# A grouped 3x3 convolution on one core: row sizes of loads and stores, whole-image stores, and semaphores cleared during the stores

## The chip, the cores and the metric

The kernel runs on one core of a Trainium2 chip. The metric is the time of one execution on the device in microseconds. Most executions of one kernel agree within about 0.3%, so a change of less than 1% needs several rounds on the same chip.

## The reference

The reference is a convolution with 16 images, 64 input channels, 128 output channels, 64 x 64 pixels, a 3 x 3 window and 8 groups, all in fp32:

```python
x_pad = np.pad(x, ((0, 0), (0, 0), (pad, pad), (pad, pad)))
for g in range(groups):                # 8 groups: 8 channels in, 16 out
    for b in range(batch):             # 16 images
        for co in range(c_out_per_group):
            for ci in range(c_in_per_group):
                for kh in range(k):
                    for kw in range(k):
                        output[b, g*16 + co] += weight[g*16 + co, ci, kh, kw] * x_pad[b, g*8 + ci, kh:kh+h, kw:kw+w]
```

It reads 16.8 MB and writes 33.6 MB.

## The kernel before

The input is loaded from GpSimd's queue with a cast from fp32 to bf16, two images to a tile of 128 partitions, 16 KB of input to a row. TensorE runs nine taps for every block of the output into PSUM. DVE and ACT evict the banks in turn into output buffers, and SyncE stores them. Two "pipes" of eight images each share TensorE. A pipe works on an image pair `i` in four sets `s`, each a quarter of both images, and the second pipe runs half a set behind the first. The prediction calls the four images that both pipes work on at a time a group. The parts that the change touches:

```python
ob = [pool.tile([128, HALF], FP32, name=f"ob{i}") for i in range(NOB)]   # NOB = 16, half images
...
for h0, h1 in ((0, 32), (32, 64)):          # the first tiles come in halves
    if h0 > 0:
        load(xn[0], 0, 0, 128, h0, h1)
    load(xs[0], 544, 0, 128, h0, h1)
    ...
    load(xs[3], 512 - 96, 96, 128, h0, h1)
for i in range(1, 4):                        # the others whole: 16 KB read per row
    load(xn[i], 128 * i, 0, 128, 0, H)
    load(xs[i], 544 + 128 * i, 0, 128 if i < 3 else 96, 0, H)
...
    def finish(self, st):                    # after a set's last tap
        i, s = st // 4, st % 4
        if s % 2 == 0:                       # a new pair of half-image buffers
            self.slots = [(nob[0] + im) % NOB for im in range(2)]
            ...
        for j in range(2):
            for im in range(2):
                ...
                eng.wait((stored[slot], 16 * uses[slot]) if uses[slot] else raw_read, self.full[j, im])
                free[b] = eng.done(copy(ob[slot][:, o0 : o0 + 512], banks[b]))
        if s % 2 == 1:
            s0 = HALF * (s // 2)
            for im in range(2):
                SP.wait(*self.wrote[im])
                nc.sync.dma_start(outf[img][:, s0 : s0 + HALF], ob[slot]).then_inc(stored[slot], 16)
...
SP.wait(*((stored[s], 16 * uses[s]) for s in range(NOB)))     # all stores landed
POOL.wait(SP.done(nc.sync.nop()))
nc.clear_and_free_semaphores(sems)
```

## Time and profile before

| | before |
|---|---|
| median time | 129.51 us (129.28 to 129.68) |
| span of the profiled execution | 127.9 us |
| TensorE busy | 86.4 us, its last eviction over at 97.5 us |
| loads end | 53 us |
| last DMA packet, last store landed | 126.1 us, 126.5 us |
| from the last landing to the end | 1.38 us |

The main lines of the page, of the DMA view and of the windows stand in the prediction. The view of waits says who waited for whom (us in total, times, longest). The evictions waited for TensorE only, never for a store to give its buffer back:

```profile
ACT ob L267 <- PE bank L240: 51.1, 33, 3.9
DVE ob L267 <- PE bank L240: 45.2, 33, 4.7
```

The chain of waits in order of time (start, duration, what) ends 30 us before the kernel does. Its last pieces:

```profile
58.98 30.89 PE bank L240 x793
89.86 0.03 issue
89.89 6.30 PE bank L240 x155
96.19 0.02 issue
96.21 1.29 DVE ob L267 x2
```

The stores that run from there on are missing from it, which is why the slice table must be read first.

### The profile page before, as it was taken

The numbers are of one execution on the slowest core, as the hardware profiler recorded it, in microseconds if no ns is written. First come the engines' busy times: TensorE is split into PE (matmuls) and PEld (weight loads), VectorE is DVE, ScalarE is ACT, GpSimd is POOL, SyncE is SP. The second block draws the span as 40 slices with busy tenths as digits, with TensorE's granted clock in tenths as the row PEclk, the third lists the DMA queues.
The fourth block names the chain that finished last, engine by engine and source line by source line (L and its number), as shares of the span: only waits on it lengthen the run. The fifth ranks groups of instructions, "written<-read, shape, count | busy, mean of one in ns | idle before, by whom it ended". The sixth has DMA issues, their size and how long they took to land.

```text
span 127.9 us, 3812 instructions
## 1 busy us (share of the span) xinstructions
PE 86.4 (68%) x2322; PEld 40.5 (32%) x1170; DVE 45.9 (36%) x74; ACT 39.0 (30%) x70; POOL 6.7 (5%) x18
## 2 busy tenths in 40 slices
PE   0029999999999979999999999999991000000000
PEld 0025435445445434553454543344340000000000
DVE  0174164456446544464544654456444000000000
ACT  4063153354345333353434533444333000000000
POOL 5950000000000000000000000000000000000000
PEclk9999999999999999999999999999999855555555
DMA  3999999999999999999999999999999999999930
GB/s 76 326 213 214 223 218 213 205 264 289 269 287 287 282 287 274 395 423 423 423 418 423 425 412 430 412 430 415 420 423 428 430 423 436 418 428 433 418 143 10
DMA packets 6271, 42.74 MB, mean 334 GB/s; under 512 B 848, under 2 KB 848, under 8 KB 1296
## 3 DMA queue, kind: packets, MB, share of 16 engines
q1 hardware_dynamic: 4752, 34.61, 65.2%
q0 software_dynamic: 1360, 7.87, 30.1%
q8 instruction: 13, 0.21, 0.6%
q10 hardware_dynamic: 144, 0.04, 0.2%
q14 instruction: 2, 0.02, 0.0%
HBM read 16.81 MB, written 33.55 MB: 394 GB/s over the span
## 4 chain that ended last, share of the span: by engine, by line
PE 66%; DVE 4%; DMA 4%; issue 1%; ACTq 0%; DVEq 0%; SPq 0%
PE bank L240 65%; DMA w_sb<-in_weight_dram 4%; DVE E L162 2%; DVE ob L267 2%; PE bank L175 2%; ACTq L329 0%; DVEq L75 0%; SPq L53 0%
## 5 line engine op out<-in xcount | busy, mean ns | idle before, releaser
L240 PE MATMUL bank<-xs,wS 32*64 32x504 bf16 (+3 forms) x1152 | 72.1, 373 | 0.9 <-issue 0.9
L240 PE MATMUL bank<-xn,wN 32*64 32x504 bf16 (+3 forms) x1152 | 70.9, 376 | 0.2 <-DVE ob L267 0.2
L267 DVE COPY ob<-bank 128x512 f32<-128x512 f32 x64 | 41.3, 686 | 45.2 <-PE bank L240 45.2
L267 ACT COPY ob<-bank 128x512 f32<-128x512 f32 x64 | 34.5, 588 | 51.1 <-PE bank L240 51.1
L235 PEld LDWEIGHTS <-wS 32*64 32x64 bf16 x576 | 27.0, 104 | 21.5 <-issue 10.9
L235 PEld LDWEIGHTS <-wN 32*64 32x64 bf16 x576 | 19.4, 105 | 24.9 <-issue 20.7
L175 PE MATMUL bank<-ident,E 128*128 128x128 bf16 x18 | 2.1, 313 | 8.8 <-DVE E L162 8.8
L175 PEld LDWEIGHTS bank<-ident,E 128*128 128x128 bf16 x18 | 1.8, 148 | 8.8 <-DVE E L162 8.8
L162 DVE TENSOR_TENSOR E<-w_sb,mask 128x288 bf16<-128x288 f32 x5 | 2.9, 653 | 4.6 <-DMA w_sb<-in_weight_dram 4.6
L106 POOL DMA_DIRECT2D xs<-in_x_dram x7 | 4.0, 571 | 1.0 <-SPq L53 1.0
L122 ACT CAST xn<-ob 128x1024 bf16<-128x1024 f32 x2 | 2.0, 1042 | 4.1 <-DMA ob<-in_x_dram 4.1
L106 POOL DMA_DIRECT2D xn<-in_x_dram x4 | 2.3, 580 | 0.0
L185 ACT CAST wS<-bank 128x512 bf16<-128x512 f32 (+1 forms) x3 | 1.2, 487 | 1.7 <-PE bank L175 1.7
L185 DVE CAST wN<-bank 128x512 bf16<-128x512 f32 (+1 forms) x3 | 1.5, 551 | 0.7 <-PE bank L175 0.7
L122 ACT ACT_TABLE_LOAD x1 | 1.3, 1283 | 1.4 <-SPq L53 1.4
L129 DVE MEMSET mask<- 128x8 f32 x1 | 0.1, 65 | 1.1 <-SPq L53 1.1
L142 POOL TENSOR_SCALAR_AFFINE_SELECT ident<-ident 128x128 bf16<-128x128 bf16 x1 | 0.3, 303 | 0.0
L137 POOL TENSOR_SCALAR_AFFINE_SELECT mask<-mask 128x8 f32<-128x8 f32 x1 | 0.2, 209 | 0.1
L147 POOL TENSOR_SCALAR_AFFINE_SELECT mask<-mask 128x8 f32<-128x8 f32 x1 | 0.2, 196 | 0.0
L315 POOL MEMSET const-float32-0.0<- 128x1 f32 x1 | 0.1, 98 | 0.3 <-issue 0.3
L130 DVE MEMSET ident<- 128x64 uint32 x1 | 0.1, 112 | 0.0
L315 POOL MEMSET const-bfloat16-1.0<- 128x1 bf16 x1 | 0.1, 101 | 0.0
(2 smaller groups left out, 0.2 us busy)
## 6 DMA issues: line engine op xcount, KB each, us to landing
out_dram<-ob SPq DMA_DIRECT2D x32, 1024.0 KB, 27.2
xn<-in_x_dram POOLq DMA_DIRECT2D x3, 1024.0 KB, 27.2
xs<-in_x_dram POOLq DMA_DIRECT2D x2, 1024.0 KB, 27.1
ob<-in_x_dram SPq DMA_DIRECT2D x1, 1024.0 KB, 5.7
xs<-in_x_dram POOLq DMA_DIRECT2D x2, 512.0 KB, 9.3
xs<-in_x_dram POOLq DMA_DIRECT2D x1, 768.0 KB, 46.0
xn<-in_x_dram POOLq DMA_DIRECT2D x1, 512.0 KB, 9.0
xs<-in_x_dram POOLq DMA_DIRECT2D x2, 128.0 KB, 9.0
```

What stands on the lines that cost most here:

```text
L106: nc.gpsimd.dma_start(t.rearrange("p h w -> p (h w)")[p0:p1, h0 * W : h1 * W], xr[row0 + p0 : row0 + p1, h0 * W : h1 * W],).then_inc(s, 16)
L122: raw_read = ACT.done(nc.scalar.copy(xn[0][:, h : h + 16, :].rearrange("p h w -> p (h w)"), raw[:, h * W : (h + 16) * W],))
L137: m3 = POOL.done(nc.gpsimd.affine_select(out=mask, in_=mask, compare_op=ALU.is_ge, fill=0.0, base=0, channel_multiplier=1, pattern=[[-COg, ...
L142: m4 = POOL.done(nc.gpsimd.affine_select(out=ident, in_=ident, compare_op=ALU.not_equal, fill=1.0, base=0, channel_multiplier=1, pattern=[ ...
L147: m5 = POOL.done(nc.gpsimd.affine_select(out=mask, in_=mask, compare_op=ALU.is_ge, fill=0.0, base=COg - 1, channel_multiplier=-1, pattern= ...
L162: e = DVE.done(nc.vector.tensor_mul(E[:, :, 32 * r : 32 * r + 32].rearrange("p t (g c) -> p t g c", c=CIg), wv.unsqueeze(2).to_broadcast([ ...
L175: ins = nc.tensor.matmul(banks[b][:, 128 * t : 128 * t + 128], E[:, t0 + t, off : off + 128], ident, start=True, stop=True,)
L185: free[b] = eng.done(copy(dst, banks[b][:, 0 : 128 * n]))
L235: pe.ldweights(w_ap, **pos)
L240: ins = pe.add_instruction(mybir.InstMatmult(name=nc.get_next_instruction_name(), engine=mybir.EngineType.PE, start_tensor_calc=k == 0, st ...
L267: free[b] = eng.done(copy(ob[slot][:, o0 : o0 + 512], banks[b]))
L315: nc = _bacc.Bacc("TRN2", target_bir_lowering=False, num_devices=1)
```

## The change

The loads of all tiles go in half images, so a row reads 8 KB and not 16. The stores go in whole images (16 KB rows), except for the first image pair of each pipe, which is still stored in halves so that stores begin early. The output buffers become eight whole images, with the same bytes. At the end, the other semaphores are cleared while the last stores are on their way; SyncE then waits for each store's semaphore and subtracts its value. TensorE's, DVE's and ACT's instructions keep their order. The intent is fewer and larger store rows, a larger share of the engines for the stores while loads run, and less to do after the last store.

```diff
--- before.py
+++ after.py
@@ -33,15 +33,14 @@
     NCH = H // R
     HALF = HW // 2
 
-    HALF = HW // 2
-    NOB = 16
+    NOB = 8
 
     pool = ctx.enter_context(tc.tile_pool(name="sb", bufs=1))
     psum = ctx.enter_context(tc.tile_pool(name="psum", bufs=1, space=bass.MemoryType.PSUM))
 
     xn = [pool.tile([128, H, W], BF16, name=f"xn{i}") for i in range(4)]
     xs = [pool.tile([128, H, W], BF16, name=f"xs{i}") for i in range(4)]
-    ob = [pool.tile([128, HALF], FP32, name=f"ob{i}") for i in range(NOB)]
+    ob = [pool.tile([128, HW], FP32, name=f"ob{i}") for i in range(NOB)]
     w_sb = pool.tile([128, CIg * T], FP32, name="w_sb")
     mask = pool.tile([128, G], FP32, name="mask")
     ident = pool.tile([128, 128], BF16, name="ident")
@@ -112,7 +111,7 @@
                 landed[t.name, q, h] = (s, 16)
 
 
-    raw = ob[NOB - 1]
+    raw = ob[NOB - 1][:, 0:HALF]
     s_raw = sem("raw")
     nc.sync.dma_start(raw, xr[0:128, 0:HALF]).then_inc(s_raw, 16)
     s_w = sem("w")
@@ -150,8 +149,9 @@
             ))
         load(xs[3], 512 - 96, 96, 128, h0, h1)
     for i in range(1, 4):
-        load(xn[i], 128 * i, 0, 128, 0, H)
-        load(xs[i], 544 + 128 * i, 0, 128 if i < 3 else 96, 0, H)
+        for h0, h1 in ((0, 32), (32, 64)):
+            load(xn[i], 128 * i, 0, 128, h0, h1)
+            load(xs[i], 544 + 128 * i, 0, 128 if i < 3 else 96, h0, h1)
 
 
 
@@ -192,7 +192,7 @@
     outf = out.rearrange("b co h w -> b co (h w)")
     taps = [(1, 1)] + [(a, b) for a in range(3) for b in range(3) if (a, b) != (1, 1)]
     pe = nc.tensor
-    stored = [sem(f"st{i}") for i in range(NOB)]
+    stored = [nc.alloc_semaphore(f"st{i}") for i in range(NOB)]
     uses = [0] * NOB
     nob = [0]
     nev = [0]
@@ -253,28 +253,29 @@
 
         def finish(self, st):
             i, s = st // 4, st % 4
-            if s % 2 == 0:
+            if s == 0:
                 self.slots = [(nob[0] + im) % NOB for im in range(2)]
+                self.empty = [(stored[slot], 16 * uses[slot]) if uses[slot] else raw_read for slot in self.slots]
                 self.wrote = [[], []]
                 nob[0] += 2
             for j in range(2):
                 for im in range(2):
                     slot, b = self.slots[im], self.banks[j][im]
-                    o0 = 512 * (2 * (s % 2) + j)
+                    o0 = 512 * (2 * s + j)
                     eng, copy = ((ACT, nc.scalar.copy), (DVE, nc.vector.tensor_copy))[nev[0] % 2]
                     nev[0] += 1
-                    eng.wait((stored[slot], 16 * uses[slot]) if uses[slot] else raw_read, self.full[j, im])
+                    eng.wait(self.empty[im], self.full[j, im])
                     free[b] = eng.done(copy(ob[slot][:, o0 : o0 + 512], banks[b]))
                     self.wrote[im].append(free[b])
                 nev[0] += 1
             nev[0] += 1
-            if s % 2 == 1:
-                s0 = HALF * (s // 2)
+            if s == 1 and i == 0 or s == 3:
+                o0, o1 = (0 if s == 1 or not (i == 0) else HALF), HALF * (s + 1) // 2
                 for im in range(2):
                     slot = self.slots[im]
                     img = 2 * i + 8 * self.k + im
                     SP.wait(*self.wrote[im])
-                    nc.sync.dma_start(outf[img][:, s0 : s0 + HALF], ob[slot]).then_inc(stored[slot], 16)
+                    nc.sync.dma_start(outf[img][:, o0:o1], ob[slot][:, o0:o1]).then_inc(stored[slot], 16)
                     uses[slot] += 1
 
     pipes = (Pipe(0), Pipe(1))
@@ -293,9 +294,20 @@
                 p.finish(st)
 
 
-    SP.wait(*((stored[s], 16 * uses[s]) for s in range(NOB)))
+
     POOL.wait(SP.done(nc.sync.nop()))
     nc.clear_and_free_semaphores(sems)
+
+    for n in range(nob[0], nob[0] + NOB):
+        s = stored[n % NOB]
+        num = dict(sync_type="semaphore", id=s.num, ant_name=s.name)
+        nc.sync.add_instruction(mybir.InstEventSemaphore(
+            name=nc.get_next_instruction_name(), engine=mybir.EngineType.SP,
+            sync_info=mybir.SyncInfo(
+                on_wait=[mybir.SyncWait(wait_mode="sem-ge-imm", wait_value=16 * uses[n % NOB], **num)],
+                on_update=[mybir.SyncUpdate(update_mode="sem-sub-imm", update_value=16 * uses[n % NOB], **num)],
+            ),
+        ))
 
 
 # ---- launch: one core; inputs and outputs as the reference has them ----
```

## The prediction

> **What bounds the kernel now.** I read the slice table first, then the DMA queues, the windows of the last microseconds, the DMA view of single stretches, and last the chain of waits. The slice table:
>
> ```profile
> PE   0029999999999979999999999999991000000000
> DMA  3999999999999999999999999999999999999930
> GB/s 76 326 213 214 223 218 213 205 264 289 269 287 287 282 287 274 395 423 423 423 418 423 425 412 430 412 430 415 420 423 428 430 423 436 418 428 433 418 143 10
> ```
>
> One slice is 3.2 us. The sixteen DMA engines are full from slice 2 to slice 38. PE is done after slice 31, and nothing but DMA runs in the last 30 us. So the kernel is bound by transfers. The chain of waits gives PE 66%, but its last piece is the eviction at 96.21 us; it does not follow the stores after that, so I don't take PE for the bound. The GB/s row counts bytes written: loads turn fp32 into bf16, so 213 written is 426 read. Loads alone fill slices 3 to 8, loads and stores share slices 9 to 16, and from slice 17 (52 us) only stores run.
>
> The queues, in packets, MB written and share of the engines' span:
>
> ```profile
> q1 hardware_dynamic: 4752, 34.61, 65.2%
> q0 software_dynamic: 1360, 7.87, 30.1%
> out_dram<-ob SPq DMA_DIRECT2D x32, 1024.0 KB, 27.2
> ```
>
> q1 is the 32 stores plus one raw load, q0 the casting loads. 65.2 + 30.1 is 95% of the span, so only the start, the end and the unevenness between engines are left over. Everything that PE, DVE and ACT do is hidden unless it leaves the DMA without work.
>
> The DMA view of 30 to 50 us shows how the two queues share:
>
> ```profile
> q0 software_dynamic: 393, 2.83, 67.6%
> q1 hardware_dynamic: 384, 2.75, 34.1%
> ```
>
> 393 packets against 384: the queues take turns packet by packet, whatever the size. A load row (16 KB read) is one packet, a store row (8 KB) is one packet, so loads get two thirds of the time.
>
> The windows of the end (DMA share and GB/s are the last two columns):
>
> ```profile
> 121.00:122.00 1.00, 0.00 (x0) 0.00 (x0) 0.00 (x0) 0.00 (x0) 0.00 (x0) 0.50 0.78 328
> 122.00:123.00 1.00, 0.00 (x0) 0.00 (x0) 0.00 (x0) 0.00 (x0) 0.00 (x0) 0.50 0.45 188
> 123.00:124.00 1.00, 0.00 (x0) 0.00 (x0) 0.00 (x0) 0.00 (x0) 0.00 (x0) 0.50 0.25 107
> 124.00:125.00 1.00, 0.00 (x0) 0.00 (x0) 0.00 (x0) 0.00 (x0) 0.00 (x0) 0.50 0.06 25
> 125.00:126.00 1.00, 0.00 (x0) 0.00 (x0) 0.00 (x0) 0.00 (x0) 0.00 (x0) 0.50 0.06 25
> ```
>
> The share falls to 0.06, one engine of sixteen. The first engines finish near 121.3 us, most by 123.9, one only at 126.1. That one sets the end. The packet records show where it fell behind: from 53.4 to 97 us its 8 KB store packets took 0.33 to 0.38 us, while most of the others took 0.309; before 53 and after 97 it was as quick as they. That is the stretch in which only stores run and the compute engines still work.
>
> **What the skill says.** "DMA: Bandwidth & Descriptors", section "Queues, rings and completion order", says an engine goes round its queues packet by packet, and that one packet may hold many descriptors; the 393 to 384 agrees with the turns, and here one row behaves as one turn. The same page, "Specifications", gives a ceiling of 435 GB/s for the sixteen engines and about 358 for HBM per core; the store-only stretch runs at 412 to 436 GB/s, so the first is the one that holds here. "Latency and other measured facts" there says that engines 7 and 15 are usually slower and guesses at the rings of GpSimd's descriptors. The trace has one slow engine but no engine numbers, and it is slow after the GpSimd loads are done, which speaks against that guess.
>
> **The change part by part.**
>
> *Stores.* 24 of the 32 half-image stores become 12 whole ones. Per engine that is 96 packets of 16 KB for 192 of 8 KB. From 100 to 120 us the trace has 1043 data packets, so one occupies 20 x 16 / 1043 = 0.307 us of an engine. At 435 GB/s 8 KB would take 0.301 us (estimate from the skill's ceiling). The overhead is then 0.006 us, and merging saves at most 96 x 0.006 = 0.5 us per engine.
>
> *Loads.* 46 rows of 16 KB per engine (368 + 368 rows over 16 engines) become 92 of 8 KB. The trace has both sizes alone: from 6 to 10 us 207 rows of 8 KB, 64 / 207 = 0.309 us each; from 15 to 22 us 183 rows of 16 KB beside one instruction fetch, 111 / 183 = 0.607 us. Two small rows cost 0.011 us more than a large one: 46 x 0.011 = +0.5 us per engine. Rows cancel: 0.0 us. GpSimd gains six issues of 0.58 us, 3.5 us while it has nothing else to do: hidden.
>
> *Sharing.* Loads were 2 to 1 ahead. Against the first group's half-image stores they are now 1 to 1. Of the loads xn2, xs2, xn3 and three quarters of xs3 are left at 24.7 us (by their landings), 3.75 x 128 rows of 16 KB: 60 small rows per engine, taking turns with the first group's 64 store packets, 60 x 0.616 = 37 us. Loads now end near 62 us, not 53. Need: the third image pair is read from about 52 us and lands by about 43; the fourth is read from about 73. No PE wait on loads. The total of DMA work does not move.
>
> *Buffers.* Eight whole-image slots hold the same bytes as sixteen halves, but a slot comes free only when its whole image has gone. Before, no eviction waited for a store. Now pipe 1 of group 2 (first eviction at 59.9 us before) needs the last slots of group 0, which come free near 60 and 64 us: DVE, ACT and then PE **stop for about 4 us**. Group 3 repeats it with about 2 us. PE ends near 102 us, not 97. This is off the path as long as stores are queued: group 1's stores are issued at 53 us, with the DMA busy on older work until 63; group 2's at 78 against 82; group 3's at about 101 against 102 for the fastest engine and some 105 for the slowest, the one that counts. So **0 us**, with little to spare.
>
> *End.* Last landing at 126.5 us, then SP's wait, a semaphore to GpSimd, its drain and a range clear of 0.22 us, the barriers, end at 127.9. The clear and one hand-over (126.66 to 127.08 us in the records) move in front of the last stores' landing; eight SP instructions of about 0.02 us replace them, seven done early. **-0.35 us.** The final barriers of the program stay.
>
> *Slow engine.* It lost about 15 packets, 4.6 us, to the fastest in 44 us. The store-only stretch with compute now runs from about 62 to 102 us, 40 us: lag down by a tenth, **-0.4 us**. If the slowness is per packet and not per byte, halving the packets takes away half the rest, 2 us. I give that a quarter: **-0.4 us** more on average.
>
> Sum: 0.0 + 0.0 - 0.35 - 0.4 - 0.4, about -1.15 us: 129.54 to **128.4 us**.
>
> **Rivals.** (a) *The wait for whole slots replaces nothing and starves the DMA.* For it: eviction, then PE, stop near 60 and 86 us, and group 3's stores come only about 1 us before the fastest engines run out. Against it: the slow engine has some 4 us more queued, and it sets the end. If the stops were 4 us longer than I work out, the time would be about 130 to 131 us. (b) *Large packets cure the slow engine.* For it: loads of 16 KB rows show no slow engine between 15 and 53 us, with compute running. Against it: those packets go the other way, and its store packets are spread over 0.33 to 0.38 us, like contention spread over bytes. It would make 126.5 to 127 us. (c) *Everything is hidden.* The bytes and the sixteen engines are the same, rows cancel, and only the end's 0.35 us shows: 129.2 us. (d) *PE as the bound.* Its last eviction is 30 us before the end; I give it nothing.
>
> **Range and chances.** Between (c) and part of (b) lies the bulk: 127.0 to 129.7 us. 2% is 2.6 us, below 126.95; only (b) in full, or with a better row rate than I read, gets there: 0.10. Over 2% slower, above 132.1, needs (a) to be much worse than worked out: 0.03.
>
> **What would show each step.** The queue view should have about 3020 packets on q1 and 2190 on q0. In 30 to 50 us the packet counts should be 1 to 1 at equal shares, and loads should end at about 62 us. Evictions should wait for stores near 60 us, and PE's last matmul come at about 101 to 103 us. The store-only rate after 103 us should be 425 to 433 GB/s. One engine should still be alone for the last 1.5 to 2.5 us. From the last landing to the end should take about 1.0 us. I am wrong if the DMA share falls under 0.9 before 120 us (rival a), or if the engines finish within 2 us of each other (rival b).

## The result and the profile after

The changed kernel takes 128.64 us (median, 128.53 to 128.73) against 129.51 us. The ratio is 0.9933, with a 95% interval of 0.9915 to 0.9952. It was run again later on another occasion: 0.9935 (0.9907 to 0.9962). So the change is faster by 0.7%, which is within 2%.

The slice table of the changed kernel (span 126.9 us, 3.17 us to a slice):

```profile
PE   0039999999999999994839999999999970000000
DMA  3999999999999999999999999999999999999970
GB/s 75 329 209 212 216 213 210 209 244 307 324 310 312 321 310 318 307 316 328 404 434 423 429 429 434 418 423 418 444 418 423 423 382 434 413 423 439 434 336 15
```

Three slices of PE are no longer full (the 4, 8 and 3 at about 57 to 67 us) and PE ends two slices later; the stretch of mixed loads and stores (307 to 328 GB/s) lasts until slice 19, not 16. In slice 33 the rate drops to 382 GB/s, which the table before has nowhere in its second half. The DMA row is otherwise as full as before. The queues, whole and from 30 to 50 us:

```profile
q1 hardware_dynamic: 3024, 34.60, 65.4%
q0 software_dynamic: 2192, 7.87, 31.4%
```

```profile
q0 software_dynamic: 575, 2.09, 51.8%
q1 hardware_dynamic: 571, 4.15, 51.4%
```

Packets alternate as before (575 to 571, sums over 100% since neighbours overlap), and with equal rows the shares are equal: it was 67.6% to 34.1%. Who waited, in the view of waits:

```profile
DVE ob L268 <- DMA out_dram<-ob: 8.0, 3, 3.4
ACT ob L268 <- DMA out_dram<-ob: 7.8, 2, 6.0
PE bank L240 <- DVE ob L268: 2.9, 4, 1.7
PE bank L240 <- ACT ob L268: 1.8, 1, 1.8
```

These waits are new: evictions wait for buffers (up to 6.0 us), and TensorE then for free banks. The windows of the stretch where the last stores are issued, and of the end (DMA share and GB/s are the last two columns):

```profile
102.00:103.00 1.00, 1.00 (x24) 0.53 (x9) 0.33 (x1) 0.07 (x1) 0.00 (x0) 1.00 0.68 279
103.00:104.00 1.00, 0.76 (x15) 0.11 (x3) 0.35 (x1) 0.39 (x1) 0.00 (x0) 1.00 1.09 459
104.00:105.00 1.00, 0.00 (x0) 0.00 (x0) 0.93 (x2) 0.69 (x2) 0.00 (x0) 1.00 0.78 328
```

```profile
121.00:122.00 1.00, 0.00 (x0) 0.00 (x0) 0.00 (x0) 0.00 (x0) 0.00 (x0) 0.50 1.11 475
122.00:123.00 1.00, 0.00 (x0) 0.00 (x0) 0.00 (x0) 0.00 (x0) 0.00 (x0) 0.50 0.77 328
123.00:124.00 1.00, 0.00 (x0) 0.00 (x0) 0.00 (x0) 0.00 (x0) 0.00 (x0) 0.50 0.35 147
124.00:125.00 1.00, 0.00 (x0) 0.00 (x0) 0.00 (x0) 0.00 (x0) 0.00 (x0) 0.50 0.08 33
125.00:126.00 1.00, 0.00 (x0) 0.00 (x0) 0.00 (x0) 0.00 (x0) 0.00 (x0) 0.50 0.00 0
```

At 102 to 105 us some engines had run dry (0.68 and 0.78): the last image group's stores came too late for the quick ones. At the end the engines finish closer together. Before, the share at 124 to 126 us was 0.06, one engine; now the last packet ends at 125.31 us, 0.8 us after the one before it, and not 2.2 us. A part of this is no gain: by the packet records the engines stood idle for 0.35 us each in the mean at 102 to 105 us, the quick ones and not the last one. In a repetition of the same kernel none stood idle, and the last packet ended 1.0 us after the next engine's.

The profile has no engine numbers, but the packets of an engine follow each other end to start, so they can be strung together from the packet records. In both kernels one engine has long store packets from the end of the loads to the end of compute: 8 KB in 0.33 to 0.38 us instead of 0.309 before, and 16 KB in a mean of 0.679 us instead of 0.611 after. I call it the **slow engine**. "Lost" below is the sum of what store packets took over 0.309 or 0.611 us, over those packets between the end of the loads and the last eviction that are 2 to 35% too long. For the changed kernel that gives 4.2 us and, in the repetition, 3.8 us; but 0.4 of the 4.2 us are packets of all engines at their restart after the idle time, from 103.2 us on, and without them both are 3.8 us.

| profiled execution, us | loads end | last eviction over | lost | mean of the 16 engines' last landings | last landing | landing to end |
|---|---|---|---|---|---|---|
| before | 53.2 | 97.5 | 4.7 | 123.1 | 126.5 | 1.38 |
| the change | 63.6 | 104.9 | 4.2 | 123.9 | 125.8 | 1.14 |
| the change, again | 62.3 | 103.6 | 3.8 | 123.3 | 125.8 | 1.14 |
| end alone | 53.3 | 97.0 | 4.7 | 122.9 | 126.2 | 1.19 |
| loads alone | 62.5 | 95.4 | 3.6 | 123.9 | 126.6 | 1.41 |
| stores alone | 54.3 | 102.4 | 4.6 | 122.5 | 126.6 | 1.34 |
| loads and stores | 62.9 | 103.2 | 3.7 | 123.2 | 125.9 | 1.36 |
| stores and end | 53.1 | 101.7 | 4.6 | 122.5 | 125.9 | 1.14 |
| all stores whole | 63.9 | 102.7 | 3.8 | 122.5 | 124.9 | 1.14 |
| all stores whole, late loads | 79.5 | 102.0 | 2.2 | 123.3 | 125.4 | 1.14 |

In the first row of the changed kernel the mean includes the idle time between 102 and 105 us (0.35 us); in the other nine rows there is none.

The loss goes with the matmuls that TensorE runs while stores run alone. Counted from the end of the loads to the last eviction (to 103.2 us in the first row of the changed kernel), it is 4.75 us for 1168 matmuls in the records before, 3.56 us for 876 with the loads alone, 3.82 us for 956 in the change again, 4.58 us for 1120 with the stores alone and 2.20 us for 567 with late loads. In all ten rows it is 3.9 to 4.1 ns for one matmul, with small store rows (4.1) as with large ones (3.9 to 4.1).

### The profile page after: what moved, and what is told of

Same layout as the page of the kernel before. It is cut to its first block, busy times and chain, and to the rows that moved or that the text cites. A ratio compares the mean times of both kernels' runs of the same rounds, so it can differ in the third digit from the quotient of the medians.

```text
span 126.9 us, 3785 instructions
## 1 busy us (share of the span) xinstructions
PE 90.4 (71%) x2322; PEld 40.4 (32%) x1170; DVE 45.9 (36%) x74; ACT 39.0 (31%) x70; POOL 9.8 (8%) x24
## 4 chain that ended last, share of the span: by engine, by line
PE 48%; DMA 27%; DVE 6%; issue 1%; ACT 0%; SPq 0%; ACTq 0%; DVEq 0%
PE bank L240 46%; DMA out_dram<-ob 24%; DVE ob L268 4%; DMA w_sb<-in_weight_dram 4%; DVE E L162 2%; PE bank L175 2%; ACT ob L268 0%; SPq L278 0%; ACTq L341 0%; DVEq L74 0%; SPq L52 0%
## 5 line engine op out<-in xcount | busy, mean ns | idle before, releaser
L240 PE MATMUL bank<-xs,wS 32*64 32x504 bf16 (+3 forms) x1152 | 75.0, 385 | 2.9 <-ACT ob L268 1.8
L240 PE MATMUL bank<-xn,wN 32*64 32x504 bf16 (+3 forms) x1152 | 74.3, 390 | 2.0 <-DVE ob L268 2.0
L105 POOL DMA_DIRECT2D xs<-in_x_dram x10 | 5.8, 578 | 1.0 <-SPq L52 1.0
L105 POOL DMA_DIRECT2D xn<-in_x_dram x7 | 4.1, 587 | 0.0
```

Source lines behind the costliest of these rows:

```text
L105: nc.gpsimd.dma_start(t.rearrange("p h w -> p (h w)")[p0:p1, h0 * W : h1 * W], xr[row0 + p0 : row0 + p1, h0 * W : h1 * W],).then_inc(s, 16)
L240: ins = pe.add_instruction(mybir.InstMatmult(name=nc.get_next_instruction_name(), engine=mybir.EngineType.PE, start_tensor_calc=k == 0, st ...
```

## The experiments

The theory: the end of the kernel is the end of its slowest engine; that engine loses a tenth of its time while stores run alone beside TensorE (theory S below); the change gains 0.2 to 0.3 us after the last landing, and the rest because that engine ends earlier. The rival: row sizes alone make the gain (theory R). Times are medians; each experiment was compared with the kernel before on the same chip in the same rounds.

### The end alone

The kernel before, with only the last hunk of the diff and `stored` taken out of the cleared semaphores.

```diff
-    SP.wait(*((stored[s], 16 * uses[s]) for s in range(NOB)))
     POOL.wait(SP.done(nc.sync.nop()))
     nc.clear_and_free_semaphores(sems)
+    for n in range(nob[0], nob[0] + NOB):
+        ...  # SP: wait for stored[n % NOB] >= 16 * uses, subtract 16 * uses
```

> Kernel before with only the end changed: the other semaphores are cleared while the stores drain, and SP waits for and subtracts each store semaphore. Theory (end plus slow engine): the time from the last landing to the end falls from 1.38 to about 1.08 us and nothing else moves: about 129.2 us, ratio 0.9977. Rival (the whole gain of 0.87 us is rows and sharing, the end was hidden behind barriers): ratio 1.000.

Measured: 129.19 us, ratio 0.9974 (0.9943 to 1.0005). In the profile the time from the last landing to the end fell from 1.38 to 1.19 us. The interval just includes 1, so the run's time alone doesn't show the gain; the records show 0.2 us, and the same step is seen wherever the new end is in (1.14 to 1.19 us against 1.34 to 1.41 us without it).

### The loads alone

The kernel before, with the hunk of the loads.

```diff
-        load(xn[i], 128 * i, 0, 128, 0, H)
-        load(xs[i], 544 + 128 * i, 0, 128 if i < 3 else 96, 0, H)
+        for h0, h1 in ((0, 32), (32, 64)):
+            load(xn[i], 128 * i, 0, 128, h0, h1)
+            load(xs[i], 544 + 128 * i, 0, 128 if i < 3 else 96, h0, h1)
```

> Kernel before with only the loads in halves (8 KB rows read). Theory S (the slow engine loses 11% only while stores run alone beside compute): loads end near 62 us instead of 53, PE still ends near 97 us, so that stretch shrinks from 44 to about 35 us and the slow engine ends about 1 us earlier; rows cost 0.5 us: about 129.0 us, ratio 0.996. Theory R (row sizes are what counts): +0.5 us, 130.0 us, ratio 1.004.

Measured: 129.33 us, ratio 0.9983 (0.9954 to 1.0013). No difference is shown. The table tells why: loads end at 62.5 us and not 53.2, the slow engine loses 3.6 us and not 4.7, but the mean engine ends 0.8 us later (123.1 to 123.9). The two cancel and the last landing stays at 126.6 us. The part of theory S about the slow engine came out (1.1 us less lost); my rows' cost of 0.5 us was rather 0.8. Theory R's +0.5 us did not show in the time.

### The stores alone

The kernel before, with whole-image buffers and stores, old loads and old end.

```diff
-            if s % 2 == 1:
-                s0 = HALF * (s // 2)
+            if s == 1 and i == 0 or s == 3:
+                o0, o1 = (0 if s == 1 or not (i == 0) else HALF), HALF * (s + 1) // 2
```

> Kernel before with only the stores changed: whole images of 16 KB rows but for the first group, eight whole-image buffers, old end. Loads keep 16 KB rows and end near 53 us. Theory S: evictions wait for stores, PE ends near 102 us, the stretch of stores beside compute grows from 44 to about 49 us, costing about 0.6 us, and large rows save about 0.5 us: 129.4 us, ratio 1.000. Theory R: only the saving of the rows, 128.9 us, ratio 0.996.

Measured: 128.94 us, ratio 0.9941 (0.9909 to 0.9974), as theory R had it. The mean engine ends 0.6 us earlier (123.1 to 122.5), which is the saving of the rows. The slow engine's loss did not change (4.7 and 4.6 us), so the 0.6 us that theory S set against the saving was not lost: the stretch is longer (48 us and not 44) because TensorE waits for buffers in it, and it runs no more matmuls there (1120 and 1168). The profiled execution was the slowest of the six (129.63 us), which is why its last landing is no better than before; the others were 0.45 to 1.1 us faster.

### Loads and stores, old end

The changed kernel with the end of the kernel before.

```diff
+    SP.wait(*((stored[s], 16 * uses[s]) for s in range(NOB)))
     POOL.wait(SP.done(nc.sync.nop()))
     nc.clear_and_free_semaphores(sems)
-    for n in range(nob[0], nob[0] + NOB): ...
```

> The changed kernel with the old end: loads in halves and stores in whole images together. Both theories: 0.3 us slower than the changed kernel, about 128.95 us, ratio 0.9956; if the end gives nothing, 128.65 us, ratio 0.9933. The queue view and the evictions' waits should be those of the changed kernel.

Measured: 128.80 us, ratio 0.9942 (0.9911 to 0.9972). The whole change gives 0.9933 and 0.9935, so the end adds less than 0.1% here. Its 0.2 us is within what the intervals leave open.

### Stores and end, old loads

The changed kernel with loads of whole images (16 KB rows) again.

```diff
-        for h0, h1 in ((0, 32), (32, 64)):
-            load(xn[i], 128 * i, 0, 128, h0, h1)
+        load(xn[i], 128 * i, 0, 128, 0, H)
```

> The changed kernel with loads of whole images again (16 KB rows read): large rows on both sides and the new end. From the run of the stores alone (mean of the 16 engines' last landings 122.5 us, against 123.2 with both) and the end's 0.2 to 0.3 us: if only the mean engine counted, 128.3 us; since the slow engine's loss of 4.2 us is kept, last landing about 126.4 us and 128.7 us, ratio 0.994, the same as the changed kernel within noise.

Measured: 128.80 us, ratio 0.9945 (0.9928 to 0.9961), as expected. The half-image loads add nothing that can be told from noise. The mean engine is 0.8 us or more earlier than in the changed kernel (122.5 us), and the last landing no earlier (125.9 us): only the slow engine counts. It loses 4.6 us here.

### Two tries to relieve the slow engine

Both start from the kernel of the section before. One half of image 15 is stored in pieces, so that not all 16 engines get the same number of rows. The Trainium skill, "DMA: Bandwidth & Descriptors", section "Why a DMA increments its semaphore by 16 and not by 1", says that the number of engines is the largest up to 16 that divides the row count, and that SyncE's transfers then take the lowest-numbered engines. The traces agree on the number: every engine that takes part writes one semaphore packet, and the first try has 23 more of them than the kernel without pieces (15 and 8), the second 34 (16, 7, 7 and 4, beside 16 as before). Which numbers the engines have, no trace shows. The first try stores 120 rows over 15 engines and 8 rows over 8:

```diff
+                    if img == 15:
+                        parts = [(0, 120, 0, HALF), (120, 128, 0, HALF), (0, 128, HALF, HW)]
```

> The kernel of big rows and new end, but of one half of image 15 only rows 0 to 119 go as one store over 15 engines and the last 8 rows over 8 engines. If the slow engine is the one that a transfer over 15 engines leaves out, it has 8 packets of 8 KB (2.5 us) less, the others at most one more (0.3 us): last landing falls from about 126.4 to about 124.3 us and the time to about 126.9 us, ratio 0.980. If it is another engine, it gets up to one packet more: last landing 126.4 to 126.8 us, 128.7 to 129.0 us, and some other engine ends 2.5 us early.

Measured: 129.64 us, ratio 1.0007 (0.9987 to 1.0027), and 128.80 us without it. The engine left out ended at 118.55 us, another one last at 126.50 us, and that one's packets show a row of the 8-row store (8 packets, a semaphore, 1 packet, a semaphore, 8 packets). So the slow engine is among the eight of the short store and isn't the one left out. The time is above my range for this case (128.7 to 129.0 us): the engine ended 1.07 us later than without pieces, of which its one packet more is 0.3 us; five of its packets between 118.0 and 123.7 us, while pieces were being stored, took 0.8 us more than usual in sum. The second try takes rows from the engines from the eighth on (96 rows over 16 engines, 21 and 7 rows over 7, 4 rows over 4):

```diff
+                    if img == 15:
+                        parts = [(0, 96, 0, HALF), (96, 117, 0, HALF), (117, 124, 0, HALF), (124, 128, 0, HALF), (0, 128, HALF, HW)]
```

> The kernel of big rows and new end, but half of image 15 is stored with 96 rows over 16 engines and 32 rows over the first 7 or 4: the engines from the eighth on have two packets of 8 KB (0.6 us) less, the first seven 2 to 3 more. The run with 15 engines showed the slow engine among the first eight. If it is the eighth, it ends 0.6 us earlier than 125.44 and the others below 124.4: 128.2 us, ratio 0.990. If it is one of the first seven, it ends 0.6 to 1.5 us later: 129.4 to 130.2 us.

Measured: 131.12 us, ratio 1.0115 (1.0080 to 1.0151). The last packet ended at 127.55 us, against 125.44 us without pieces, and the last engine's packets between semaphores are 6, 3, 1 and 8, with a single packet once, where four other engines have two (1, 1 and 8 at the end): it took part in the stores over seven engines, and not in the 4-row store. The guess that it is the eighth was wrong. It got two packets of 0.309 us more, 0.6 us, and ended 2.1 us later. The other part lies in its packets too: between 118.2 and 124.8 us six of them took 0.04 to 0.5 us longer than usual, 1.4 us in sum. On all engines 50 packets of 8 KB were over 0.312 us from 116 us on, up to 1.03 us, while the kernel without pieces has none over 0.614 us for 16 KB from 105 us on. So splitting the store itself stretched packets; by what way is not shown. The run was slower than both of my expectations. But it shows, on correct output, that work given to this one engine goes straight into the time, while the other fifteen end before 124.5 us.

The windows of this run's end; a share of 0.06 is again one engine:

```profile
124.00:125.00 1.00, 0.00 (x0) 0.00 (x0) 0.00 (x0) 0.00 (x0) 0.00 (x0) 0.50 0.10 41
125.00:126.00 1.00, 0.00 (x0) 0.00 (x0) 0.00 (x0) 0.00 (x0) 0.00 (x0) 0.50 0.06 25
126.00:127.00 1.00, 0.00 (x0) 0.00 (x0) 0.00 (x0) 0.00 (x0) 0.00 (x0) 0.50 0.08 33
127.00:128.00 1.00, 0.00 (x0) 0.00 (x0) 0.00 (x0) 0.00 (x0) 0.00 (x0) 0.50 0.02 8
```

### A third of the taps (wrong)

The changed kernel with three of nine taps, so a third of TensorE's matmuls and weight loads, with all evictions and transfers.

```diff
+            if k not in (0, 1, T - 1):
+                return
```

> Wrong on purpose: the changed kernel with 3 of 9 taps, so a third of TensorE's matmuls and weight loads with all evictions and transfers. It asks what slows the one engine while stores run alone. If it is TensorE's instructions or reads, its store packets fall from about 0.68 us to 0.63 or less while compute goes on; if it is the evictions' writes, they stay at 0.66 to 0.69 us as long as evictions run and go to 0.611 after. Either way PE is done sooner (by about 90 us, held by the buffers) and the last landing comes at 123 to 125.5 us.

Measured: 126.46 us (one run), last packet at 123.24 us, with evictions going on to 103.7 us. Two windows near the end of compute, and two of the end:

```profile
102.00:103.00 1.00, 0.00 (x0) 0.00 (x0) 1.00 (x2) 1.00 (x3) 0.00 (x0) 0.50 0.27 115
103.00:104.00 1.00, 0.00 (x0) 0.00 (x0) 0.68 (x2) 0.21 (x1) 0.00 (x0) 0.50 0.66 279
122.00:123.00 1.00, 0.00 (x0) 0.00 (x0) 0.00 (x0) 0.00 (x0) 0.00 (x0) 0.50 0.65 279
123.00:124.00 1.00, 0.00 (x0) 0.00 (x0) 0.00 (x0) 0.00 (x0) 0.00 (x0) 0.50 0.01 0
```

All sixteen engines end between 123.06 and 123.24 us. That says nothing about their speed before: at 102 to 104 us all had run dry (0.27 and 0.66), the slow one too, and they began the last stores together. What counts is the packets before. Strung together, one engine still has long ones: 45 store packets between 69 and 97 us with a mean of 0.634 us (about the 0.63 that I had set), against 0.611 us for the quick ones and 0.679 us in the changed kernel. So its excess fell from 0.068 to 0.023 us, to a third, as TensorE's work did, while all evictions were still there; the evictions' writes can account for a third at most. Its loss of 1.35 us up to 103.2 us for 292 matmuls is 4.6 ns for one, near the 3.9 to 4.1 ns of the correct runs. Two other things changed too, and I can't take them apart from it: there were 4 instruction fetches by DMA in place of 13, and the granted clock was 0.58.

### As many instructions, less data (wrong)

The changed kernel, with all matmuls after the first tap reading one row of the image instead of 7 or 8.

```diff
+            if k > 0:
+                hi = lo + 1
```

> Wrong on purpose: the changed kernel with as many TensorE instructions, but all matmuls beyond the first tap read one row of 64 instead of 7 or 8. If the slow engine is slowed by TensorE's stream of instructions, its store packets stay at 0.67 us or more while stores run alone beside TensorE, and 13 instruction fetches remain; if it is the data that TensorE reads or writes, they fall to about 0.61 to 0.63 us, as with 3 of 9 taps, and all engines end within 0.5 us of each other but for the fetches.

Measured: 129.03 us (one run), last packet at 125.63 us, 1.0 us after the next engine. One engine had a mean of 0.652 us per 16 KB packet between 67 and 97 us, between the two cases that I had set: it comes in bursts, a packet of 0.80 to 0.86 us between some of 0.62 to 0.65. There were 13 instruction fetches again, and the granted clock was 0.62, so a low clock alone does not leave that engine as quick as the rest. Its loss was 1.6 us for 744 matmuls, 2.2 ns for one, about half of that in the correct runs: so it seems that neither all nor none of it goes with the data. The run doesn't decide between TensorE's stream of instructions and its data. It is **open** by what way TensorE slows that engine.

### All stores whole

The changed kernel, with the first image pair also stored in whole images, so that stores begin later.

```diff
-            if s == 1 and i == 0 or s == 3:
-                o0, o1 = (0 if s == 1 or not (i == 0) else HALF), HALF * (s + 1) // 2
+            if s == 3:
+                o0, o1 = 0, HALF * (s + 1) // 2
```

> The changed kernel with the first group also stored in whole images: no store before 33 us. If only the sum of DMA work and the slow engine count, the loads alone keep the engines full until 33 us, loads and group 0 are both done at about 63 us as before, and the time stays within 0.4 us of the changed kernel, 128.3 to 129.0 us. If early stores matter (slots later free, DMA without work), it is over 130 us.

Measured: 128.23 us, ratio 0.9909 (0.9885 to 0.9932), just below the range that I had set (128.3 to 129.0 us). Stores that begin 9 us later (the first is issued at 31.0 us, not at 22.0 or 22.5) cost nothing, since loads keep the engines full meanwhile. The slice table:

```profile
DMA  3999999999999999999999999999999999999960
GB/s 76 330 211 218 212 211 213 217 212 212 213 324 376 335 370 346 351 357 378 408 434 429 421 437 416 426 426 416 437 426 426 421 426 437 432 426 437 421 270 26
```

Loads alone run through slice 11, and the last load ends at 63.9 us, as in the changed kernel (63.6). Its early stores in half images were not needed. The loads have 8 KB rows here too, and yet the mean engine ends at 122.5 us, 0.8 us earlier than in the repetition of the changed kernel. Its whole first stores explain some 0.2 us of that (estimate: large rows saved 0.6 us for 96 merged packets, and 32 more are merged here). So most of the 0.8 us of the loads alone is not the price of small load rows by themselves: it was there where these rows took turns with stores in half images. Why, no run shows.

### All stores whole, the last image pair loaded in quarters

If the slow engine loses only while stores run alone beside TensorE, loads that last longer should help. The last image pair's loads go in quarter images (4 KB rows read against 16 KB store rows).

```diff
+        n = 32 if i < 3 else 16
-        for h0, h1 in ((0, 32), (32, 64)):
+        for h0, h1 in ((h, h + n) for h in range(0, H, n)):
```

> The kernel with whole-image stores for all groups, and the last image pair loaded in quarters (4 KB rows read, against 16 KB store rows, so the loads get a fifth of the engines). Theory (the slow engine loses time only where stores run alone while TensorE works): loads end at about 77 us instead of 64, that stretch shrinks from about 40 to 27 us, the slow engine's loss from 3.7 to about 2.4 us; small rows cost 0.3 us; last landing about 124.0 us, time about 127.3 us, ratio 0.983. Rival (the slow engine loses per byte stored, wherever): loss stays at 3.7 us and the small rows make it slower, 128.6 us, ratio 0.993.

Measured: 128.33 us (127.36 to 128.78), ratio 0.9878 (0.9838 to 0.9918). From 40 to 60 us the queues shared as worked out:

```profile
q1 hardware_dynamic: 458, 6.72, 80.4%
q0 software_dynamic: 458, 0.82, 21.7%
```

Loads ended at 79.5 us, and the slow engine lost 2.2 us and not 3.8 as with the same stores and earlier loads, as the theory has it; the rival's 3.7 us did not come. But the time did not fall to 127.3 us. The mean engine ends at 123.3 us against 122.5 without the quarters, and in the profiled run the last engine ended at 124.97 us with the next at 124.60, 124.35 and 124.26 us. The slow engine no longer stands apart, and the others, some with an instruction fetch or two of 0.9 us, are the next limit. The changed kernel, run again in the same rounds:

> The changed kernel once more, on the same chip and in the same rounds as the three beside it: ratio 0.9933 as the first time, 0.991 to 0.996.

Measured: 128.87 us, ratio 0.9935 (0.9907 to 0.9962). Both kernels with all stores whole are faster than before by 0.9 and 1.2%, and their means are below the changed kernel's; their intervals against the kernel before overlap with its. The kernel with late loads ran in the same rounds as the changed one: the means are 128.16 and 128.86 us, 0.7 us apart (95% interval 0.1 to 1.3, six runs each), so its gain is shown, if barely. That of all stores whole alone was not compared in the same rounds; it is likely and not shown.

## Why the prediction was right or wrong

- **The bound.** Right. DMA is full in both but for the idle time at 102 to 105 us, and TensorE's last eviction ended 6 to 7 us later and cost nothing.
- **Stores, -0.5 us.** Right. The stores alone gave -0.5 us by the medians and -0.8 us by the ratio (0.9941), and 0.6 us on the mean engine.
- **Loads, +0.5 us.** On the mean engine it was rather 0.8 us, and hardly for the reason given (a price of each small row): with the same loads and no half-image stores, most of it was gone. In the time of the loads alone it did not show, because the slow engine lost 1.1 us less.
- **Sharing.** Right: 575 packets to 571 at equal shares, and loads ended at 63.6 and 62.3 us against 62.
- **Buffers, 0 us.** The stops came (longest 6.0 us for ACT, 4 us expected), TensorE's last eviction ended at 104.9 and 103.6 us. The margin of 1 us for the fastest engines was too small in one of two profiles: the share fell to 0.68 at 102 us, so what I had named as a sign of rival (a) did appear; in the repetition no engine ran dry. It cost nothing for the reason given there: the slow engine still had work from the group before, and it sets the end.
- **End, -0.35 us.** Direction right, size 0.24 us (1.38 to 1.14 us).
- **Slow engine, -0.4 us.** Right in direction, too small: it lost 3.8 us and not 4.7, so -0.9 us. I had taken the loss by time, 40 us for 44. It goes by TensorE's matmuls in that stretch, and these fell from 1168 to 956, because loads ended 10 us later while a part of the stretch is TensorE's waiting.
- **A quarter chance of large packets curing it, -0.4 us more.** This did not happen. The slowed packets took 1.12 times the usual time at 8 KB (0.347 us for 0.309) and at 16 KB (0.682 us for 0.611): a packet of twice the bytes lost almost twice as much, so the loss does not go by packets. A quarter of the 2 us named would also have been 0.5 and not 0.4 us.
- **One engine alone for the last 1.5 to 2.5 us.** It was 0.8 and 1.0 us.

With the measured sizes the sum is -0.6 + 0.8 - 0.24 - 0.9, about -0.9 us, and -0.87 us was measured; -1.15 us was predicted. So the total was near partly by luck: the cure that did not come and rows that did not cancel were nearly made up for by the slow engine's larger gain.

What is shown is that one engine sets the end (what two runs put on it, or stretched there, came out in the time), that its loss goes with the matmuls beside lone stores (ten profiles, and one with a third of the taps) and shrinks when loads last longer, and that large store rows carry most of the change's gain (0.9941 alone, and 0.9945 with the end, of 0.9933). By the ratios the parts do not add up: 0.3 + 0.2 + 0.8 us alone against 0.87 us together, within intervals of 0.3 to 0.4 us each way. Why TensorE slows one engine is not settled.

## What to carry to other kernels

When DMA is full throughout, look at how the sixteen engines finish: a share of 0.06 in the last microseconds is one engine, and only what that engine gains counts. Before you take an equal finish for equal speed, look if the engines ran dry and started again together. Here two queues took turns row by row, so row sizes set how loads and stores shared the engines; this moved when each ended, and cost no time in these runs as long as the slow engine had work. Before adding early small transfers to start a queue sooner, ask if the engines are idle then: here the plainer kernel with whole stores throughout was no slower.

## What the Trainium skill lacked or had wrong

- "DMA: Bandwidth & Descriptors", "Latency and other measured facts": it names engines 7 and 15 as usually slower and guesses at GpSimd's descriptor rings. Here the slow engine took part in the stores over seven engines and not in the one over four, so by the page's own rule it is one of the seven lowest-numbered, the first four excepted, and neither 7 nor 15. It was slow after GpSimd's loads were done, by a factor of 1.12 on the slowed rows of 8 and 16 KB. The page has nothing on what its loss goes with here: 3.9 to 4.1 ns for each matmul that ran beside lone stores, in ten profiles.
- The same page, "Queues, rings and completion order": it gives 9 to 17 descriptors as typical for a packet, and does not say there how rows of some KB are packed. Here two queues alternated row by row: 393 to 384 packets with 16 KB against 8 KB rows, 575 to 571 with 8 KB against 8 KB, 458 to 458 with 4 KB against 16 KB (shares 21.7 and 80.4%).
- No page has what a store waits when another queue keeps the engines full: the first store was issued at 22.05 us and its first packet ran at 25.60 us before, 22.47 and 26.41 us after; SyncE's one load, on idle engines, was issued at 1.02 us and ran at 2.09 us. In the changed kernel load packets stretched from 0.324 to as much as 0.79 us meanwhile.
- No page has a number for what one store in pieces costs the engines: with 5 stores in place of one, the last engine's end moved by 2.1 us, 0.6 us of it for two more packets and 1.4 us for packets that were stretched while the pieces ran.
